# The first seven-product pair of a macaron block's feed-forward layer: two weight chunks fetched ahead into idle tiles, modulation rows fetched later, a shorter look-ahead

## The chip, the cores and the metric

The kernel runs on one core of one Trainium2 chip. A core has five instruction engines here: TensorE (PE in the profile, with its weight loads as PEld), VectorE (DVE), ScalarE (ACT), GpSimd (POOL) and SyncE (SP), which only issues transfers. Each engine takes its instructions strictly in the order of its own list, and waits on semaphores for the others. The metric is the device time of one execution in microseconds (us).

## The reference, cut to what matters

One transformer block on 512 tokens of width 1024, in float32. The change lies in the first of its three sub-layers, a SwiGLU feed-forward layer behind a modulated RMSNorm:

```
mod = silu(c) @ w_ada + b_ada                  # nine rows of 1024: shift, scale, gate, three times
u = modulate(rmsnorm(h, g_norm_ffn1), sh1, sc1)
a, b = split(u @ w_ffn1_in, 2)                 # 1024 -> 2 x 2816
h = h + 0.5 * gt1 * ((silu(a) * b) @ w_ffn1_out)
...                                            # token mixing, with gt2
...                                            # the second feed-forward layer, with gt3
return rmsnorm(h, g_final)
```

## The kernel before

**Tiles.** The hidden width 2816 is cut into 22 tiles of 128 columns, numbered j. Tile j needs 128 columns of the a half and 128 of the b half of `w_ffn1_in`. The layer runs in parts: tiles 0 to 3 are multiplied with `w_ffn1_out` first, then 4 to 7, and so on. Tiles 0 to 5 are made by plain products. From tile 6 on, two tiles (a pair) are made together by `duo`, as one 2 by 2 block product with seven block products in place of eight: the two halves of the width and the two halves of the tokens (T1, T2) are the blocks, some operands are sums and differences of blocks, and the seven results are combined in the banks A, B and C of PSUM. Pair 6 (tiles 6 and 7) is the first of them. Its products stand right behind the output products of part 0, and pair 8 follows.

**High and low parts.** A weight chunk (128 x 1024, 512 KB) is loaded raw, and then split: ACT rounds it into `whi` (line 321), DVE subtracts that from it into `wlo` (line 335). Each product is three groups of matmuls: high weights with high data, high with low, and last low weights with high data. A chunk listed in `self.outer` has its low part made in another way, which spares DVE: ACT writes the negated rounded chunk into `wlo` (line 317), and a transfer issued by POOL adds the chunk from memory onto it (line 319, `accum_op`). I call that an adding transfer. `whi` and `wlo` are rings of about seven chunks.

**The seven weights of a pair.** Four raw chunks r11, r12, r22, r21 are loaded in that order, and seven operands are made from them in place, in two buffers X besides; I number them w0 to w6:

```
for need, src, make in ((0, r11, None), (1, x0, (x0, r12, r11)), (2, x1, (x1, r22, x0)), (3, r21, None),
                        (3, r12, (r12, r22, r12)), (3, r22, None), (3, x0, (x0, r21, x1))):
```

The subtractions (`make`) are DVE's, at line 260. For pair 6, w0, w3 and w5 are listed in `self.outer`; for the later pairs w3 and w5 only.

**The buffers.** `fetch` hands a free buffer to the next chunk of the list and issues its load on SP's queue (line 244); `split` goes through the list up to a given place; `look(ahead)` does both for the current place plus `ahead`. At first there are three raw buffers. A buffer is free again when the last operand that is made from it has been split. The X buffers of pair 6 are still in use by the sums of the data (`u_steps`, tiles X, SH, SL: a list `todo` of seven steps, one behind each update of H in the output loop of part 0), and only then, when `todo` is empty, `hold` is dropped and w1 and w2 are made.

**Modulation rows.** `bg` consumes one row of `w_ada` (line 389) at places between the products, and `bg_fetch` issues the loads of the rows ahead (line 381), into the tiles `ada` at first, and from part 0's output products on into `cs` and `AR`. The rows 16 to 23 make the gate of this layer, which multiplies every output before it is added to H.

**In `duo`.** Before each product `look` is called, the product is issued, then what follows it: behind the first product ACT copies bank A into bank C (line 776), since A goes on to be accumulated and both are needed; behind that, the last data block is split (`first()`: UH, UL). `later(n, f)` puts f behind the n-th product from now; `ffn_post` uses it for the first token half of tiles 4 and 5 (line 677, 678), which nobody needs before part 1's outputs.

Of the kernel before, what the change touches and what calls it, by code (L numbers as in the profile page):

```python
# [8 lines left out]
F32 = mybir.dt.float32  # L9
F32R = mybir.dt.float32r  # L10
I32 = mybir.dt.int32
AF = mybir.ActivationFunctionType
OP = mybir.AluOpType

P = 128
T = 512
HT = 256
D = 1024
# [124 lines left out]
class Kernel:  # L143
# [6 lines left out]
    def plan(self):  # L150
        (i1, o1), mix, (i2, o2) = chunk_widths()
        self.chunks = []
        for name, ws in (("wf1i", i1), ("wf1o", o1), ("wmix", mix), ("wf2i", i2), ("wf2o", o2)):
            off, rec = 0, []
            for w in ws:
                rec.append((name, off, w))
                off += P * w
            self.chunks.append(rec)
        f1i, f1o, mx, f2i, f2o = self.chunks


        self.loads, self.order, self.last = [], [], {}
        self.shifted, self.outer, self.tail = set(), {}, []

        def plain(recs):
            for r in recs:
                n = len(self.loads)
                self.loads.append(r)
                self.last[n] = len(self.order)
                self.order.append((r[2], n, ("raw", n), None))  # L170

        def blocks(recs, outer=0, rest=()):
            n = len(self.loads)
            if outer > 1:
                self.outer.update({len(self.order) + 3: n + 3, len(self.order) + 5: n + 2})
            if outer in (1, 3):
                self.outer[len(self.order)] = n
            self.shifted.update(range(len(self.order), len(self.order) + 7 + len(rest)))
            self.loads.extend(recs)
            r11, r12, r22, r21 = (("raw", n + i) for i in range(4))  # L180
            x0, x1 = ("x", 0), ("x", 1)
            for need, src, make in ((0, r11, None), (1, x0, (x0, r12, r11)), (2, x1, (x1, r22, x0)), (3, r21, None),
                                    (3, r12, (r12, r22, r12)), (3, r22, None), (3, x0, (x0, r21, x1))):
                if rest and make == (x0, r21, x1):
                    self.tail.append(len(self.order))
                    plain(rest)
                for j, x in enumerate((r11, r12, r22, r21)):
                    if x == src or (make and x in make):
                        self.last[n + j] = len(self.order)
                self.order.append((D, n + need, src, make))  # L190

        def shift(i):

            self.shifted.update(range(len(self.order) - i, len(self.order)))

        def ffn(n, ins, outs, first):
            j, at = first, 0
            if first:
                plain(ins[:KT])
                at = KT  # L200
            for part, (k0, k1) in enumerate(PARTS):
                while j < pairs_before(n, part):
                    if j < PLAIN[n]:
                        plain(ins[at:at + 2])
                        if n and j < 2:
                            shift(2)
                        j, at = j + 1, at + 2
                    else:
                        blocks(ins[at:at + 4], 2 if j > PLAIN[n] else 3)
                        j, at = j + 2, at + 4  # L210
                recs = outs[part * KT // 2:(part + 1) * KT // 2]
                if part + 1 == len(PARTS):
                    continue
                if n or part:
                    blocks(recs, (3, 0, 2)[n], outs[-2:] if part + 2 == len(PARTS) else ())
                else:
                    base = len(self.order)
                    plain(recs)
                    self.outer.update({base + i: self.order[base + i][1] for i in (2, 3)})

        ffn(0, f1i, f1o, FIRST)
        base = len(self.order)
        plain(mx)
        self.shifted.update(range(base, base + 4))
        self.outer.update({i: self.order[i][1] for i in (base + 2, base + 3)})
        shift(2)
        ffn(2, f2i, f2o, 0)
        self.fetched = self.done = self.made = 0
        self.pos, self.held, self.retired, self.half, self.hold = 0, None, [], None, True
        self.at, self.start, self.top = {}, {}, 0  # L230
        self.buf = {}
        self.units = {base + i: 2 * P for i in (4, 5)}
        self.units.update({base + i: T for i in range(16, 20)})
# [434 lines left out]
    def ffn_post(self, j, s, pb, between=None):  # L668
        nc = self.nc
        h = self.kept[j // 2 % 3][:, j % 2 * T:j % 2 * T + T]  # L670
        nc.vector.tensor_tensor(h, s, pb, op=OP.mult)
        hh, hl = self.hh(j)
        t = slice(0, HT)
        if self.nh == 6 and j < 2:
            hh, hl, h = hh[:, t], hl[:, t], h[:, t]
        if self.nh == 4 and j in (4, 5):
            self.later(5, lambda: nc.scalar.activation(hh[:, t], h[:, t], AF.Copy))
            self.later(6, lambda: nc.vector.tensor_tensor(hl[:, t], h[:, t], hh[:, t], op=OP.subtract))
            return
        nc.scalar.activation(hh, h, AF.Copy)  # L680
        low = lambda: nc.vector.tensor_tensor(hl, h, hh, op=OP.subtract)
        if between is None:
            return low()
        between(low)
# [88 lines left out]
    def duo(self, j, first):  # L773

        nc, v = self.nc, self.nc.vector
# [5 lines left out]
        for i in range(3):  # L781
            h, l = self.S[i]
# [23 lines left out]
        for i, (bank, u, start) in enumerate(((A, blk(lo4, T1), True), (B, S[0], True), (A, S[1], False),  # L806
                                              (C, blk(hi4, T1), False), (A, S[2], False), (B, S[3], False),
                                              (A, blk(hi4, T2), False))):
            if i == 6:
                v.tensor_tensor(c1, c1, u3, op=OP.add)  # L810
            self.look(3 + i // 3 if first and self.nh == 6 else 5)
            self.product(bank, u, start)
            self.step()
            if i == 0:
                copy(C, A)
                if first:
                    first()
                    self.free.append(self.rawx[0])
            elif i == 1:
                copy(c1, r(B))  # L820
            elif i == 2:
                copy(c0, r(A))
            elif i == 3:
                silu(0, C)
            elif i == 4:
                copy(u3, r(A))
            elif i == 6:
                silu(1, A)
                v.tensor_tensor(c0, r(B), c0, op=OP.add)
            self.beside(j, i)  # L830
            if self.nh == 4 and j >= PARTS[-2][0] and self.todo:
                self.todo.pop(0)()
# [306 lines left out]
    def ffn(self, n, j, last=None):  # L1139
# [12 lines left out]
        for part, (k0, k1) in enumerate(PARTS[:-1]):  # L1152
            while j < pairs_before(n, part):
                if j < PLAIN[n]:
                    self.ffn_pair(j, beside)
                    j += 1
                else:
                    if j == k1:
                        if n and part == 0:
                            self.open_G()  # L1160
                        self.h_sums(k0, 0 if n else 4)
                    self.duo(j, last)
                    last = None
                    j += 2
# [18 lines left out]
            nk = k1 - k0  # L1183
            hk = [self.hh(k) for k in range(k0, k1)]
            for m in range(0, KT, 2):
                self.look(4 - m // 2)
                w = self.take()
                bs = [self.nb(), self.nb()]
# [18 lines left out]
    def beside_out(self, part):  # L1207

        if part == 0:

            assert not self.adat
            self.ada_pool.close()
            self.ada_free, self.ada_stop = [self.cs, self.AR], 40
            self.bg_fetch()
            self.sums = self.open_sums()
            self.open_G()
            self.todo, last = self.u_steps(0)
            return last
        if part == len(PARTS) - 2:
            assert self.ada_next == 40 and not self.adat, self.ada_next  # L1220
            self.ada_free = None
            self.retired = self.rawx
            self.free = [b for b in self.free if not any(b is x for x in self.rawx)]
            assert not self.todo
            self.trig_spread()
        if part == 2:
            self.todo = self.trig()
# [641 lines left out]
```

## Time and profile before

| what | value |
|---|---|
| time, median of 3 runs (lowest to highest) | 997.5 us (995.49 to 997.6) |
| the profiled execution: its own time, and its span from first to last instruction | 996.86 us, 995.1 us |
| granted TensorE clock, mean over the span | 0.993 |
| PE busy | 977.1 us (98%) |
| DVE busy | 829.1 us (83%) |
| ACT busy | 592.6 us (60%) |
| POOL busy | 97.2 us (10%) |
| transfers | 173.29 MB, mean 174 GB/s |

A row of a timeline or of the chain of waits begins with its start in microseconds from the span's start, then its duration. L770 is the matmul line of the block products, L366 to L368 are those of the plain ones. In the timeline, what stands in brackets at the end is the idle time of the engine just before the row, and who ended it. A row with x8 is eight instructions in a run.

### The profile page before, as it was taken

To read this page: it belongs to the slowest core of one execution; us is meant where nothing else is said; L and a number is where in the kernel's file an instruction comes from. 1 tells how busy PE (TensorE), PEld (TensorE's weight loads), DVE (VectorE), ACT (ScalarE), POOL (GpSimd) and SP (SyncE) were. 2 spreads that over 40 slices of the span, in tenths; PEclk is the share of its full clock that TensorE was granted. 3 is DMA by queue.
4 is the path that set the end of the run, shared out by engine and by line. 5 is a ranking of instruction groups with operands and counts; after the bars stand their busy time and mean duration, and the time that the engine had idled before them with its cause. 6 is when DMAs were issued, how large, how long until landed. Compare 5 with 4: busy or idle time off the path is not lost.

```text
span 995.1 us, 17672 instructions
## 1 busy us (share of the span) xinstructions
PE 977.1 (98%) x7106; PEld 920.1 (92%) x7106; DVE 829.1 (83%) x1244; ACT 592.6 (60%) x912; POOL 97.2 (10%) x109
## 2 busy tenths in 40 slices
PE   8999799999999999999999999999999999999997
PEld 6888799999999999889988888899999999999996
DVE  6976899999999876879667777579997988989875
ACT  6453577776868853334324333368776768677775
POOL 0001111111111100006300000001110011011001
PEclk9999899999999999999999999999999999999998
DMA  9869597777869723232255874345576666657632
GB/s 341 277 210 277 129 274 187 231 221 172 233 189 245 193 70 100 70 105 88 95 200 187 284 236 162 106 149 129 148 166 182 162 153 168 188 134 188 173 59 85
DMA packets 53924, 173.29 MB, mean 174 GB/s; under 512 B 6097, under 2 KB 11217, under 8 KB 53842
## 3 DMA queue, kind: packets, MB, share of 16 engines
q1 hardware_dynamic: 41778, 137.95, 40.3%
q0 software_dynamic: 11376, 33.56, 20.2%
q8 instruction: 55, 0.90, 0.4%
q10 hardware_dynamic: 688, 0.66, 0.2%
q14 instruction: 27, 0.22, 0.1%
HBM read 169.37 MB, written 2.77 MB: 173 GB/s over the span
## 4 chain that ended last, share of the span: by engine, by line
PE 90%; DVE 5%; ACT 2%; DMA 2%; issue 1%; DVEq 0%; ACTq 0%; SPq 0%
PE bank L770 34%; PE bank L366 7%; PE bank L368 7%; PE bank L367 7%; PE bank L890 6%; PE bank L892 6%; PE bank L891 6%; PE bank L632 3%; PE bank L1799 1%; PE bank L1801 1%; PE bank L1803 1%; PE bank L1389 1%; DMA ada<-wada 1%; PE bank L1570 1%; PE bank L1571 1%
## 5 line engine op out<-in xcount | busy, mean ns | idle before, releaser
L321 ACT ACTIVATE whi<-raw 128x1024 fp32r<-128x1024 f32 (+5 forms) x166 | 145.5, 896 | 9.6 <-DVE raw L260 5.0
L335 DVE TENSOR_TENSOR wlo<-raw,whi 128x1024 fp32r<-128x1024 f32 (+5 forms) x114 | 119.1, 1058 | 38.4 <-ACT whi L321 38.1
L321 ACT ACTIVATE whi<-X 128x1024 fp32r<-128x1024 f32 (+3 forms) x102 | 97.9, 973 | 31.1 <-DVE X L260 30.7
L335 DVE TENSOR_TENSOR wlo<-X,whi 128x1024 fp32r<-128x1024 f32 (+1 forms) x76 | 86.9, 1149 | 12.8 <-ACT whi L321 12.7
L366 PE MATMUL bank<-UH,whi 128*128 128x512 f32 x240 | 97.4, 406 | 0.0
L368 PE MATMUL bank<-UH,wlo 128*128 128x512 f32 x240 | 93.6, 390 | 0.0
L367 PE MATMUL bank<-UL,whi 128*128 128x512 f32 x240 | 93.5, 390 | 0.0
L770 PE MATMUL bank<-UH,whi 128*128 128x256 f32 x576 | 77.3, 277 | 0.0
L770 PE MATMUL bank<-UL,whi 128*128 128x256 f32 x576 | 77.2, 276 | 0.0
L770 PE MATMUL bank<-UH,wlo 128*128 128x256 f32 x576 | 77.2, 276 | 0.0
L770 PEld LDWEIGHTS bank<-UH,whi 128*128 128x128 f32 x576 | 71.1, 188 | 0.1
L770 PEld LDWEIGHTS bank<-UH,wlo 128*128 128x128 f32 x576 | 70.8, 188 | 0.0
L770 PEld LDWEIGHTS bank<-UL,whi 128*128 128x128 f32 x576 | 70.8, 188 | 0.0
L890 PE MATMUL bank<-HI,whi 128*128 128x256 f32 x240 | 66.8, 278 | 0.0
L891 PE MATMUL bank<-HK,whi 128*128 128x256 f32 x240 | 66.4, 277 | 0.0
L892 PE MATMUL bank<-HI,wlo 128*128 128x256 f32 x240 | 66.4, 277 | 0.0
L770 PE MATMUL bank<-SH,whi 128*128 128x256 f32 x432 | 59.2, 280 | 5.7 <-ACT bank L776 3.6
L389 DVE SCALAR_TENSOR_TENSOR ada<-ada,cond 128x1024 f32<-128x1024 f32 (+1 forms) x49 | 57.5, 1198 | 8.2 <-DMA ada<-wada 8.2
L770 PEld LDWEIGHTS bank<-SH,whi 128*128 128x128 f32 x432 | 53.9, 190 | 6.4 <-ACT bank L776 3.8
L890 PE MATMUL bank<-ut,whi 128*128 128x256 f32 x216 | 59.7, 277 | 0.0
L891 PE MATMUL bank<-G,whi 128*128 128x256 f32 x216 | 59.7, 277 | 0.0
L892 PE MATMUL bank<-ut,wlo 128*128 128x256 f32 x216 | 59.7, 277 | 0.0
(365 smaller groups left out, 2638.7 us busy)
## 6 DMA issues: line engine op xcount, KB each, us to landing
ada<-wada SPq DMA_DIRECT2D x47, 512.0 KB, 5.5
raw<-wmix SPq DMA_DIRECT2D x44, 512.0 KB, 4.4
raw<-wf1i SPq DMA_DIRECT2D x31, 512.0 KB, 6.9
raw<-wf2i SPq DMA_DIRECT2D x27, 512.0 KB, 5.2
wlo<-wf2i POOLq DMA_DIRECT2D x20, 512.0 KB, 6.0
AR<-wada SPq DMA_DIRECT2D x16, 512.0 KB, 4.0
raw<-wf1o SPq DMA_DIRECT2D x15, 512.0 KB, 5.4
X<-wf2i SPq DMA_DIRECT2D x14, 512.0 KB, 6.4
```

The lines of the kernel that those rows point to most:

```text
L321: self.nc.scalar.activation(self.hi[:, y], r[:, x], AF.Copy)
L335: self.nc.vector.tensor_tensor(self.lo[:, y], r[:, x], self.hi[:, y], op=OP.subtract)
L366: M(ps, hi, uh, start=start, stop=False)
L367: M(ps, hi, ul, start=False, stop=False)
L368: M(ps, lo, uh, start=False, stop=stop)
L389: self.nc.vector.scalar_tensor_tensor(t[:, c], t[:, c], 1.0, self.cond[:, c], op0=OP.mult, op1=OP.mult, accum_out=o)
L632: M(banks[j][:, hs], w[j][k][x], (self.UH, self.UL)[y][k][:, hs], start=h == k == x == y == 0, stop=k == KT - 1 and x == 1, skip_group_che ...
L770: M(bank[:, p * HT:(p + 1) * HT], w[4 * p + k][x], u[k][y], start=start and x == y == p == k == 0, stop=x == 1 and k == 3, skip_group_chec ...
L890: M(o, hi, uh, start=start and m % 2 == 0 and k == 0, stop=False, skip_group_check=True)
L891: M(o, hi, ul, start=False, stop=False, skip_group_check=True)
L892: M(o, lo, uh, start=False, stop=k == 1, skip_group_check=True)
L1389: M(o, pt[:, blk * P:blk * P + P], v, start=i == 0, stop=i == len(srcs) - 1)
```

## The change

Five edits, all at or around pair 6:

1. The third output chunk of part 0 is no longer in `self.outer`: its low part is made by DVE.
2. While the output products of part 0 run, two more buffers are handed out for raw chunks: `kept[1]`, whose tiles 2 and 3 have been used by then, and the first 1024 columns of tile G, which is opened for its own use (`open_G`) only when pair 8 begins. Being `retired`, they are given back after one use.
3. `bg_fetch` for the rows 24 and 25 (into `cs` and `AR`) moves from the beginning of that loop to its third step (m = 4).
4. The look-ahead in pair 6 is 3, 3, 3, 4, 4, 4, 5 chunks for its seven products in place of 5 for each.
5. The splits of tiles 4 and 5 (first token half) move two products back.

```diff
@@ plan: the output chunks of part 0
-                    self.outer.update({base + i: self.order[base + i][1] for i in (2, 3)})
+                    self.outer[base + 3] = self.order[base + 3][1]
@@ ffn_post
         if self.nh == 4 and j in (4, 5):
-            self.later(5, lambda: nc.scalar.activation(hh[:, t], h[:, t], AF.Copy))
-            self.later(6, lambda: nc.vector.tensor_tensor(hl[:, t], h[:, t], hh[:, t], op=OP.subtract))
+            self.later(7, lambda: nc.scalar.activation(hh[:, t], h[:, t], AF.Copy))
+            self.later(8, lambda: nc.vector.tensor_tensor(hl[:, t], h[:, t], hh[:, t], op=OP.subtract))
@@ duo
-            self.look(3 + i // 3 if first and self.nh == 6 else 5)
+            self.look(3 + i // 3 if first else 5)
@@ ffn, ahead of pair 8
-                        if n and part == 0:
+                        if part == (0 if n else 1):
                             self.open_G()
@@ ffn, the output loop of part 0
             for m in range(0, KT, 2):
+                if m == 4:
+                    self.bg_fetch()
                 self.look(4 - m // 2)
@@ beside_out
             self.ada_free, self.ada_stop = [self.cs, self.AR], 40
-            self.bg_fetch()
             self.sums = self.open_sums()
-            self.open_G()
+            self.retired = [self.kept[1], self.fw.tile([P, 3 * T], F32, name="G")[:, :D]]
+            self.free.extend(self.retired)
```

What this does to the instructions shows best on two engines. The first is SP's queue, from the last output chunk of part 0 (wf1o) on; wf1i are the chunks of pair 6 and then of pair 8, wada the modulation rows. Before:

```order
L244 DMA raw0_66<-wf1o 128x1024
L381 DMA ada_632<-wada 128x1024
L381 DMA ada_635<-wada 128x1024
L244 DMA raw1_67<-wf1i 128x1024
L381 DMA ada_670<-wada 128x1024
L244 DMA raw2_68<-wf1i 128x1024
L381 DMA cs_93<-wada 128x1024
L381 DMA AR_86<-wada 128x1024
L244 DMA raw0_66<-wf1i 128x1024
L244 DMA raw1_67<-wf1i 128x1024
L244 DMA X_123<-wf1i 128x1024
```

and now, from the last gate row on:

```order
L381 DMA ada_668<-wada 128x1024
L244 DMA raw2_68<-wf1i 128x1024
L244 DMA raw0_66<-wf1i 128x1024
L244 DMA kept1_121<-wf1i 128x1024
L244 DMA G_721<-wf1i 128x1024
L381 DMA cs_93<-wada 128x1024
L381 DMA AR_86<-wada 128x1024
L244 DMA raw1_67<-wf1i 128x1024
```

r21, the fourth chunk of pair 6, went into raw1 behind r11, which had to be used up first; now it goes into `kept1`, and r11 of pair 8 into G. The rows for `cs` and `AR` stand behind the four chunks.

The second is ACT around the first product of pair 6. Before, from the high parts of w1 and w2 on (`whi<-X`, two in a row):

```order
L321 ACTIVATE whi_69<-X_123 128x1024 x2
L317 ACTIVATE wlo_70<-raw1_67 128x1024
L321 ACTIVATE whi_69<-raw1_67 128x1024
L321 ACTIVATE whi_69<-raw2_68 128x1024
L677 ACTIVATE HI_118<-kept2_122 128x256 x2
L776 ACTIVATE bank6_103<-bank4_101 128x512
L736 ACTIVATE UH_81<-X_123 128x4x256
L317 ACTIVATE wlo_70<-raw0_66 128x256
L317 ACTIVATE wlo_70<-raw0_66 128x768
```

and now:

```order
L317 ACTIVATE wlo_70<-kept1_121 128x1024
L321 ACTIVATE whi_69<-kept1_121 128x1024
L776 ACTIVATE bank6_103<-bank4_101 128x512
L736 ACTIVATE UH_81<-X_123 128x4x256
L321 ACTIVATE whi_69<-raw2_68 128x1024
L776 ACTIVATE kept0_120<-bank5_102 128x2x256
L317 ACTIVATE wlo_70<-raw0_66 128x256
L317 ACTIVATE wlo_70<-raw0_66 128x768
L321 ACTIVATE whi_69<-raw0_66 128x256
L321 ACTIVATE whi_69<-raw0_66 128x768
L677 ACTIVATE HI_118<-kept2_122 128x256 x2
```

The copy of bank A into bank C (bank6 from bank4) now has only the two instructions of w3 between itself and the high parts of w1 and w2; the high part of w4 (from raw2) and the two splits of tiles 4 and 5 have moved behind it. TensorE's list is the same before and after, matmul for matmul.

## The prediction

> **What bounds the kernel now.** I read the page first, then PE's waits, then PE's timeline at the place where it waits. The page: who is busy, and PE's busy tenths in 40 slices of 24.9 us.
>
> ```profile
> PE 977.1 (98%) x7106; PEld 920.1 (92%) x7106; DVE 829.1 (83%) x1244; ACT 592.6 (60%) x912; POOL 97.2 (10%) x109
> PE   8999799999999999999999999999999999999997
> ```
>
> PE is the bound nearly everywhere; only the first, the fifth and the last slice show a hole. The fifth (99.5 to 124.4 us) holds the first products of pair 6. The waits of PE between 60 and 200 us, and the timeline there (start, duration):
>
> ```profile
> PE bank L770 <- ACT bank L776: 3.6, 1, 3.6
> PE bank L770 <- ACT whi L321: 2.1, 1, 2.1
> ...
> 101.20 0.39 PE L368 MATMUL bank<-HI,wlo 128*128 128x512 f32 x1
> ...
> 104.14 1.10 PE L770 MATMUL bank<-UH,whi 128*128 128x256 f32 x8
> 106.03 1.10 PE L770 MATMUL bank<-UH,wlo 128*128 128x256 f32 x8
> 109.21 1.19 PE L770 MATMUL bank<-SH,whi 128*128 128x256 f32 x8 [2.08 <-ACT whi L321]
> 111.19 1.09 PE L770 MATMUL bank<-SH,wlo 128*128 128x256 f32 x8
> 115.86 2.08 PE L770 MATMUL bank<-SH,whi 128*128 128x256 f32 x8 [3.58 <-ACT bank L776]
> 121.14 1.16 PE L770 MATMUL bank<-UH,whi 128*128 128x256 f32 x8
> ```
>
> A product is 24 matmuls. The first runs from 104.14 to 107.13, the second, after a wait of 2.08 for the high part of w1, from 109.21 to 112.28, the third, after 3.58 for the copy of bank A, from 115.86 to 121.14. What three products should take stands in the chain of waits, where 336 of them run unbroken:
>
> ```profile
> 79.59 12.34 DMA ada<-wada
> 92.02 1.24 DVE ada L389 x2
> ...
> 105.02 0.66 DVE H L1197
> ...
> 106.85 1.24 DVE X L260
> 108.15 3.42 DMA raw<-wf1i
> ...
> 170.41 38.19 PE bank L770 x336
> ```
>
> 38.19 / 336 is 0.1137 us for a matmul, 2.73 for a product, 8.19 for three. They took 17.00 (104.14 to 121.14). So **8.81 us is all that there is to win here**: 2.08 and 3.58 of waiting, 2.55 in the third product (5.28 in place of 2.73), and 0.6 in the first two (2.99 and 3.07). Why the third took twice its time is in the busy times of two stretches of 6.83 us (PE, PEld, DVE, ACT, POOL, then the granted clock):
>
> ```profile
> 107.63:114.45 6.82, 3.06 (x24) 2.87 (x24) 5.82 (x6) 4.92 (x5) 0.87 (x1) 1.00 0.44 154
> 114.45:121.28 6.83, 5.42 (x25) 5.42 (x26) 5.22 (x6) 6.78 (x12) 1.76 (x2) 0.50 0.91 183
> ```
>
> After a stretch in which PE worked 3.06 of 6.82 us, half the clock was granted for the next. Shorter waits take that away too.
>
> The same chain says who is late. The last row of the gate lands 12.34 us after its issue, DVE takes it at 92.02, and from then on DVE works without a break through the updates of H and the sums of the data up to 106.85, where it makes w1; the buffer that this frees lets r21 be loaded at 108.15, and ACT, in its order, waits for it:
>
> ```profile
> 108.11 1.06 ACT L321 ACTIVATE whi<-X 128x1024 fp32r<-128x1024 f32 x1 [5.58 <-DVE X L260]
> 109.42 1.06 ACT L321 ACTIVATE whi<-X 128x1024 fp32r<-128x1024 f32 x1 [0.26 <-DVE X L260]
> 111.65 1.06 ACT L317 ACTIVATE wlo<-raw 128x1024 fp32r<-128x1024 f32 x1 [1.17 <-DMA raw<-wf1i]
> 112.62 2.09 ACT L321 ACTIVATE whi<-raw 128x1024 fp32r<-128x1024 f32 x2
> 114.62 0.70 ACT L677 ACTIVATE HI<-kept 128x256 fp32r<-128x256 f32 x2
> 115.23 0.58 ACT L776 ACTIVATE bank<-bank 128x512 f32<-128x512 f32 x1
> 115.74 1.03 ACT L736 ACTIVATE UH<-X 128x1024 fp32r<-128x1024 f32 x1
> 116.68 1.14 ACT L317 ACTIVATE wlo<-raw 128x256 fp32r<-128x256 f32 x2
> ```
>
> **The change part by part.** *The adding transfer that goes (edit 1).* The two queues of the page, plain loads and adding transfers: packets, MB, share of all 16 transfer engines.
>
> ```profile
> q1 hardware_dynamic: 41778, 137.95, 40.3%
> q0 software_dynamic: 11376, 33.56, 20.2%
> DVE ada L389 <- DMA ada<-wada: 8.2, 3, 4.4
> ```
>
> 20.2% of 995.1 us for 33.56 MB is 5.99 us per MB: 0.524 MB cost 3.14 us of all engines, where a plain chunk costs 1.52. One such transfer, ahead of the last gate row, goes, so the row should land 3.1 us earlier. Bounds: 0 (it stood behind other traffic) and the 3.3 from which the output products hold DVE: the bank of H's seventh update is done at 101.59 (101.20 + 0.39), and w1 begins 1.83 behind that update (105.02 to 106.85), at 103.5 at best. I take 3.1: w1 at 103.75. DVE pays one more low part, at most 1.3 us in two pieces, while it waits up to 4.4 at a time for these rows (the third row above, from DVE's waits of 58 to 155 us): nothing. Without that cover it would be 1.3 of the 3.1, and 1.8 would be left.
>
> *First wait.* The high part of w1 ends 2.32 after DVE begins w1 (106.85 to 109.17): at 106.07, before PE is through with the first product (107.13). The 2.08 go. That holds as long as the row gains 2.08.
>
> *Second wait (edits 2, 4, 5).* r21 is loaded into `kept1`, straight behind r22, long before its use: ACT's 1.17 go. The high part of w2 starts 2.57 behind w1 (106.85 to 109.42), at 106.32, and ends at 107.38; the two instructions of w3 stand at 0.97 each (111.65 to 112.62), so the copy of bank A starts at 109.24 and ends at 109.82. PE, starting the second product at 107.13 with its 3.07, is through at 110.20: 0.38 to spare, the 3.58 go. If the row gains only 2.08, the copy ends at 110.84, and 0.7 stay. What moved behind the copy: w4's high part, then starting near 110.7, needed at 115.9; the splits of tiles 4 and 5, needed by part 1's outputs alone. w1's and w2's low parts are DVE's next:
>
> ```profile
> 109.25 2.50 DVE L335 TENSOR_TENSOR wlo<-X,whi 128x1024 fp32r<-128x1024 f32 x2
> ```
>
> They end 4.9 behind w1, at 108.65; w2's low third is due at 112.0. Four more instructions of 1.25 at most lie between that and w4's low part, at about 113.7, due at 117.7.
>
> *What is late next.* The low parts of w3 and w5 come by adding transfers, and these do not move up as far as PE does. POOL's issues of both in the trace (first and last start), and the times to landing of each; last those of all 44 and more up to 345 us:
>
> ```profile
> L319 POOL DMA_DIRECT2D wlo<-wf1i x1: 872/872/872, 113.1 to 113.1; - x1
> DMA to landing us min/median/max: 5.3/5.3/5.3
> ...
> L319 POOL DMA_DIRECT2D wlo<-wf1i x2: 865/943/1021, 117.4 to 118.2; - x2
> DMA to landing us min/median/max: 5.9/7.3/8.7
> ...
> DMA to landing us min/median/max: 2.9/6.8/10.5
> ```
>
> w3: issued 0.4 after ACT's instruction (111.65 + 1.06 = 112.71 to 113.1). Now that instruction runs from 107.30 to 108.36, so the issue is at 108.7, the landing at 114.0, or 115.0 if the two loads released by w1 (3.42 each) overlap it by a microsecond. The fourth product starts at 110.20 + 2.73 = 112.93, its last third at 114.75. I take a wait of 0.2; bounds 0 (2.9) and 4.45 (10.5).
>
> w5: behind the copy ACT splits UH (to 110.7), w4 (to 111.7), copies a bank (to 112.2) and then does w5's two pieces; POOL issued the second 1.5 behind ACT's start (116.68 to 118.2), now at 113.7, and 8.7 later, at 122.4, it lands. PE begins the sixth product at 115.86 + 2.73 = 118.6 and needs that piece at its third low matmul, at 120.65. **A new wait of 1.75**; bounds 0 (2.9) and 3.55 (10.5). I take 8.7, since that is this very transfer.
>
> [...]
>
> *Modulation rows later (edit 3).* `cs` and `AR` went behind the last gate row, so they don't delay it either way; their landing is due only at the first `bg` of pair 6. 0; a late landing would hold DVE there.
>
> *The clock.* Two waits of 0.2 and 1.75 leave PE at work for well over 3.06 of any 6.83 us; I take no halving. If the waits reach the 3.76 us idle of the row above, it is 2.55 more.
>
> *Later.* The gain must survive to the end. Busy times from pair 8's end to the end of the layer:
>
> ```profile
> 151.00:345.00 194.00, 194.00 (x1712) 194.00 (x1711) 183.14 (x236) 148.64 (x215) 30.76 (x35) 1.00 0.79 208
> ```
>
> PE has no hole, DVE is at 94%, so an earlier start goes through.
>
> **The sum**: 2.08 + 3.58 + 2.55 + 0.60 = 8.81, less 0.60 (the slow pace of the first two products, which nothing in the change touches), 0.2 and 1.75: 6.26. The profiled execution took 996.86 us (span 995.1), which makes 990.6; the median shown is 0.64 higher, so I say 990.8.
>
> **The rivals.** (B) *Full recovery*: w5's transfer lands in 6.8, the median, or less: 8.81 - 0.6 = 8.2, 988.7. For it: with four chunks loaded ahead, fewer loads compete; against: both pieces wait in one queue, behind each other. [...]
> (C) *The gate row lands no earlier*, so the edit's main step does nothing: w1 stays at 106.85 and the 2.08 stay; the copy comes 3.1 later than above, at 112.92, 0.6 after the second product; w5's piece at 125.5 against 123.2: 2.3. Gain 8.81 - 0.6 - 2.08 - 0.6 - 2.3 = 3.2: 993.6. For it: the row's 12.34 us are shared with other traffic, an adding transfer among it that stays.
> (D) *The adding transfer of w3 takes the longest time seen*, 10.5: 4.45 of wait, half the clock again (2.55), nothing left for w5: gain 1.2, 995.7.
> (E) *Slower*, by the same transfer alone: at 14 us from issue the wait is 7.95, with 2.55 and 0.6 that is 11.1 against 8.81: 999.1. It decides from about 13.7 us; the longest row is 10.5, which speaks against it.
>
> **How the numbers follow.** 0.2% (2 us) is about what can be told from no change. The forecast of 990.8 (989.5 to 992.5 for bounds of half a wait) gets 0.57, B 0.17, C 0.13, D 0.07, E 0.03, other things 0.03. Range 988.0 to 994.6: it takes in B and C and leaves out D and E. Faster: forecast, B and C, and a little of D, 0.89; within 0.2%: the rest of D, 0.07; slower 0.04.
>
> **What would show it.** In the new profile the chain has no load of wf1i between w1 and pair 6's products; DVE takes the last gate row near 89; the 2.08 and 3.58 are gone, and no half clock stands near 115. A wait of one to two microseconds on a POOL transfer stands in the sixth product, near 120.7; pair 6 ends near 125.8 in place of 132.1. The prediction is wrong if that row does not move, if the copy of bank A still ends a wait, or if a wait of over 3 us stands at w3 or w5.

## The result, and the profile after

The changed kernel takes 990.64 us, the median of seven runs (988.7 to 993.53), against 997.05 (994.84 to 997.84) for the kernel before on the same chip: a ratio of 0.994, with a 95% interval of 0.992 to 0.996. The forecast was 990.8, in a range of 988.0 to 994.6.

The page of the profiled execution, whose own time was 993.37 us and its span 991.6, shows who was busy, PE's tenths, and the queue of the adding transfers:

```profile
PE 977.8 (99%) x7106; PEld 921.3 (93%) x7106; DVE 830.4 (84%) x1246; ACT 591.5 (60%) x910; POOL 95.6 (10%) x107
PE   8999999999999999999999999999999999999997
q0 software_dynamic: 11088, 33.04, 19.7%
```

The hole in the fifth slice is gone, and the adding queue moves 0.52 MB less. PE's waits between 60 and 200 us, and its timeline in pair 6 (the first rows of products one to four, then the whole sixth and the first row of the seventh) show what is left there:

```profile
PE bank L770 <- DMA wlo<-wf1i: 1.7, 1, 1.7
...
107.09 1.10 PE L770 MATMUL bank<-UH,whi 128*128 128x256 f32 x8
...
109.92 1.10 PE L770 MATMUL bank<-SH,whi 128*128 128x256 f32 x8
...
112.74 1.07 PE L770 MATMUL bank<-SH,whi 128*128 128x256 f32 x8
...
115.46 1.07 PE L770 MATMUL bank<-UH,whi 128*128 128x256 f32 x8
...
121.00 1.07 PE L770 MATMUL bank<-UH,whi 128*128 128x256 f32 x8
121.91 1.07 PE L770 MATMUL bank<-UL,whi 128*128 128x256 f32 x8
122.82 0.39 PE L770 MATMUL bank<-UH,wlo 128*128 128x256 f32 x2
124.95 0.96 PE L770 MATMUL bank<-UH,wlo 128*128 128x256 f32 x6 [1.75 <-DMA wlo<-wf1i]
125.75 1.07 PE L770 MATMUL bank<-UH,whi 128*128 128x256 f32 x8
...
128.47 0.73 PE L770 MATMUL bank<-UH,whi 128*128 128x256 f32 x5
```

The two waits of 2.08 and 3.58 are gone; the third product takes 2.72 (112.74 to 115.46) where it took 5.28. One wait stands there that was not there before: 1.75 us, in the sixth product, behind two low matmuls. The seven products end at 128.47, 21.38 us after they began; before they took 27.97 (104.14 to 132.11).

Pair 6 starts 2.95 us later than in the profile before, though. That has nothing to do with the change; it lies in the first 20 us, ahead of everything that was edited. PE's timeline there, before:

```profile
11.51 1.22 PE L1733 MATMUL bank<-ones,ut 128*128 128x1 f32 x8
...
15.18 1.50 PE L1728 MATMUL bank<-H,ones 128*128 128x128 f32 x12
16.93 2.14 PE L1799 MATMUL bank<-UH,whi 128*128 128x512 f32 x8 [0.25 <-ACT UH L486]
```

and after, with the same instructions two lines further down in the code:

```profile
11.56 1.71 PE L1735 MATMUL bank<-ones,ut 128*128 128x1 f32 x8
...
17.53 2.67 PE L1730 MATMUL bank<-H,ones 128*128 128x128 f32 x12
19.95 2.08 PE L1801 MATMUL bank<-UH,whi 128*128 128x512 f32 x8
```

Twelve matmuls that took 1.50 take 2.67. In the 14 profiles of this study (kernel before, changed kernel, and twelve runs below) the large matmuls begin between 16.2 and 17.6 us in nine, and between 19.5 and 20.0 in five. One kernel, the last of the table below, was profiled twice and had both (16.24 and 19.57). So the whole time of a single execution says little about a few microseconds. What follows goes by a stage: from the first matmul of pair 6 to the first one of part 1's outputs, fourteen block products in all. **It took 47.06 us before and takes 40.63 now, 6.43 less.** From there to the end of the span it is 843.88 and 843.87: what the stage gained went through to the end, as far as two decimals show.

Why the waits went is in the rows of DVE and ACT. DVE takes the last gate row and makes w1 and w2; ACT makes what follows:

```profile
89.68 1.23 DVE L389 SCALAR_TENSOR_TENSOR ada<-ada,cond 128x1024 f32<-128x1024 f32 x1 [1.56 <-DMA ada<-wada]
...
104.58 0.75 DVE L1199 SCALAR_TENSOR_TENSOR H<-bank,mod,H 128x512 f32<-128x512 f32 x1 [0.84 <-PE bank L368]
...
106.50 1.23 DVE L260 TENSOR_TENSOR X<-raw,raw 128x1024 f32<-128x1024 f32 x1
...
107.75 1.06 ACT L321 ACTIVATE whi<-X 128x1024 fp32r<-128x1024 f32 x1 [7.57 <-DVE X L260]
...
110.04 1.04 ACT L317 ACTIVATE wlo<-kept 128x1024 fp32r<-128x1024 f32 x1
110.99 1.05 ACT L321 ACTIVATE whi<-kept 128x1024 fp32r<-128x1024 f32 x1
111.93 0.58 ACT L776 ACTIVATE bank<-bank 128x512 f32<-128x512 f32 x1
```

DVE now waits for PE ahead of an update of H (0.84): it has caught up with the output products, and w1 starts 0.59 before pair 6 does (106.50 against 107.09), where it started 2.71 after it. r21 stands ready in `kept`, so ACT goes from w2 to w3 and to the copy of bank A without a wait; the copy ends at 112.51, 0.23 before the third product starts.

### The profile page after: what moved, and what is told of

It is laid out like the page before. It is cut to its first block, busy times and chain, and to the rows that moved or that the text cites. A ratio compares the mean times of both kernels' runs of the same rounds, so it can differ in the third digit from the quotient of the medians.

```text
span 991.6 us, 17667 instructions
## 1 busy us (share of the span) xinstructions
PE 977.8 (99%) x7106; PEld 921.3 (93%) x7106; DVE 830.4 (84%) x1246; ACT 591.5 (60%) x910; POOL 95.6 (10%) x107
## 4 chain that ended last, share of the span: by engine, by line
PE 94%; DVE 3%; ACT 1%; DMA 1%; issue 0%; DVEq 0%; ACTq 0%
PE bank L770 33%; PE bank L366 8%; PE bank L368 8%; PE bank L367 8%; PE bank L890 6%; PE bank L892 6%; PE bank L891 6%; PE bank L632 3%; PE bank L1801 1%; PE bank L1805 1%; PE bank L1803 1%; PE bank L1391 1%; PE bank L1572 1%; DMA wlo<-wf1i 1%; PE bank L1730 1%; PE bank L1573 1%
## 5 line engine op out<-in xcount | busy, mean ns | idle before, releaser
L335 DVE TENSOR_TENSOR wlo<-raw,whi 128x1024 fp32r<-128x1024 f32 (+5 forms) x117 | 121.6, 1053 | 38.4 <-ACT whi L321 38.1
L335 DVE TENSOR_TENSOR wlo<-X,whi 128x1024 fp32r<-128x1024 f32 (+1 forms) x74 | 84.5, 1148 | 11.9 <-ACT whi L321 11.8
L770 PE MATMUL bank<-UH,wlo 128*128 128x256 f32 x576 | 77.5, 277 | 1.7 <-DMA wlo<-wf1i 1.7
L770 PE MATMUL bank<-UH,whi 128*128 128x256 f32 x576 | 77.2, 276 | 0.0
L770 PE MATMUL bank<-UL,whi 128*128 128x256 f32 x576 | 77.2, 276 | 0.0
L770 PEld LDWEIGHTS bank<-UH,wlo 128*128 128x128 f32 x576 | 70.9, 188 | 1.9 <-DMA wlo<-wf1i 1.9
L770 PEld LDWEIGHTS bank<-UH,whi 128*128 128x128 f32 x576 | 70.9, 188 | 0.1
L770 PEld LDWEIGHTS bank<-UL,whi 128*128 128x128 f32 x576 | 70.8, 188 | 0.0
L770 PE MATMUL bank<-SL,whi 128*128 128x256 f32 x432 | 58.5, 278 | 0.0
L770 PE MATMUL bank<-SH,whi 128*128 128x256 f32 x432 | 58.3, 277 | 0.0
```

Of the source, the lines that this page charges most:

```text
L335: self.nc.vector.tensor_tensor(self.lo[:, y], r[:, x], self.hi[:, y], op=OP.subtract)
L770: M(bank[:, p * HT:(p + 1) * HT], w[4 * p + k][x], u[k][y], start=start and x == y == p == k == 0, stop=x == 1 and k == 3, skip_group_chec ...
```

## The experiments

Twelve runs, told in the order of the questions: what each edit is worth, what the wait that is left hangs on, and what it takes to remove it. The table has the time of the stage, the waits of PE in it, and for how long half the clock was granted there; each time is from one profile.

| kernel | stage, us | waits of PE, us | half clock, us |
|---|---|---|---|
| before | 47.06 | 2.08, 3.58 | 6.83 |
| changed | 40.63 | 1.75 | 0 |
| changed, profiled again | 42.35 | 2.00 | 3.41 |
| edit 1 taken back | 44.17 | 0.80, 0.63, 1.82 | 3.41 |
| edit 1 alone | 44.43 | 3.06 | 6.83 |
| edit 2 taken back | 41.95 | 0.98, 1.58 | 0 |
| edit 3 taken back | 40.63 | 1.53 | 0 |
| edits 4 and 5 taken back | 42.69 | 2.61 | 3.41 |
| edit 4 taken back | 42.71 | 1.99, 0.2 | 3.41 |
| edit 5 taken back | 43.07 | 0.27, 2.09 | 3.41 |
| w5 by DVE | 42.37 | 2.20, in pair 8 | 3.41 |
| two modulation rows later | 40.81 | 1.92 | 0 |
| both of these | 38.55 and 39.08 | none | 0 |

**Edit 1 taken back**: the third output chunk of part 0 gets its low part by an adding transfer again.

```diff
-                    self.outer[base + 3] = self.order[base + 3][1]
+                    self.outer.update({base + i: self.order[base + i][1] for i in (2, 3)})
```

> The changed kernel with edit 1 taken back: the third output chunk of part 0 gets its low part by an adding transfer again. Measured is the time from the first matmul of pair 6 to the first of part 1's outputs (pairs 6 and 8): 47.06 us before, 40.63 in the changed kernel. My theory (three waits, each with a cause of its own): the last gate row lands late again, w1 is made about 3 us later, the wait of about 2.1 ahead of the second product comes back, with 0.5 to 0.7 ahead of the third and some 0.5 more at w5: 43 to 44.5 us. Rival (the early load of r21 is all that counts): 40.6 us, with no wait ahead of the second product.

44.17. The last gate row's issue on SP's queue with its time to landing, then the start of w1 on DVE's timeline, and PE's waits in the stage:

```profile
L381 SPq DMA_DIRECT2D ada<-wada x1: 330/330/330, 79.4 to 79.4; - x1
DMA to landing us min/median/max: 11.1/11.1/11.1
...
105.33 1.23 DVE L260 TENSOR_TENSOR X<-raw,raw 128x1024 f32<-128x1024 f32 x1
...
PE bank L770 <- DMA wlo<-wf1i: 1.8, 1, 1.8
PE bank L770 <- ACT whi L321: 0.8, 1, 0.8
PE bank L770 <- ACT bank L776: 0.6, 1, 0.6
```

The row takes 11.1 us to land (12.34 before); in the changed kernel the slowest of the last three took 7.0. w1 starts 1.41 behind pair 6's start (103.92), in place of 0.59 ahead of it, and the first wait is back. It is 0.8 and not 2.1, since w1 is still 1.30 earlier against PE than before: without edit 1 the other edits bring that much, and which of them isn't shown. So 44.17 lies in my range by another sum, with 1.3 less in the first wait and with 3.41 us at half the clock, 1.7 us, which I hadn't counted. Rival C of the prediction (the row lands no earlier by this) falls.

**Edit 1 alone**, on the kernel before.

```diff
-                    self.outer.update({base + i: self.order[base + i][1] for i in (2, 3)})
+                    self.outer[base + 3] = self.order[base + 3][1]
```

> The kernel before with edit 1 alone. My theory, from the prediction's terms: the last gate row lands some 3 us earlier relative to pair 6, so the wait of 2.08 for the high part of w1 goes, but r21 still comes late into its buffer and ACT's copy of bank A behind it: the second wait stays at 3 to 4.5 us, with slow matmuls behind it or not: 44 to 45.5 against 47.06. Rival C of the prediction, for this edit by itself: the row lands no earlier and the time stays within 0.4 of 47.06.

44.43, with one wait, for the copy of bank A. PE's waits, and ACT's row for w3 from its timeline:

```profile
PE bank L770 <- ACT bank L776: 3.1, 1, 3.1
...
109.49 1.06 ACT L317 ACTIVATE wlo<-raw 128x1024 fp32r<-128x1024 f32 x1 [1.73 <-DMA raw<-wf1i]
```

The first wait is gone and the second stays, as the terms of the prediction have it: ACT still waits 1.73 for r21. The last gate row lands in 6.54 us here, and w1 starts at 104.11, 0.6 ahead of pair 6 (104.72), as in the changed kernel: edit 1 alone does the whole of that step.

**Edit 2 taken back** (r21 and r11 of pair 8 wait for buffers again).

```diff
-            self.retired = [self.kept[1], self.fw.tile([P, 3 * T], F32, name="G")[:, :D]]
-            self.free.extend(self.retired)
```

> The changed kernel with edit 2 taken back: no extra buffers, so r21 waits again until w1 has used up r11; the order on ScalarE stays the new one. My theory: the load goes out about 0.7 us behind the start of pair 6 and lands 3.4 later, ScalarE does w3's two instructions from 4.2 on, the copy of bank A ends at 6.7 and the third product, due at 5.65, waits 1.1 us, with as much more at w3's or w5's low part: 41.5 to 43 us for pairs 6 and 8. Rival (the early load is all that counts): the wait of 3.6 us and the half clock come back, 46 us or more.

41.95, with waits of 0.98 at the copy of bank A and 1.58 at w5, by PE's waits:

```profile
PE bank L770 <- DMA wlo<-wf1i: 1.6, 1, 1.6
PE bank L770 <- ACT bank L776: 1.0, 1, 1.0
```

The wait at the copy is near the 1.1 that I expected; the one at w5 is no longer than in the changed kernel. The stage is 1.32 longer, so the buffers are worth about a microsecond, and the rival falls: no half clock comes back.

**Edits 4 and 5 taken back** (look-ahead of 5, the splits of tiles 4 and 5 two products earlier).

```diff
-            self.look(3 + i // 3 if first else 5)
+            self.look(3 + i // 3 if first and self.nh == 6 else 5)
...
-            self.later(7, lambda: nc.scalar.activation(hh[:, t], h[:, t], AF.Copy))
...
+            self.later(5, lambda: nc.scalar.activation(hh[:, t], h[:, t], AF.Copy))
...
```

> The changed kernel with edits 4 and 5 taken back: look-ahead 5 in pair 6, the splits of tiles 4 and 5 at their old place; the two extra buffers stay. My theory: the copy of bank A stands behind w4's high part again, which needs a subtraction that VectorE does not finish before about 6.1 us behind the start of pair 6, and behind the two splits: it ends near 8.3, the third product waits about 2.7 us; 42 to 43.3 us for pairs 6 and 8. Rival (the early load of r21 is all that counts): 40.6 us.

42.69, and one wait of 2.61. ACT's rows ahead of the copy:

```profile
113.07 1.06 ACT L321 ACTIVATE whi<-raw 128x1024 fp32r<-128x1024 f32 x1 [1.28 <-DVE raw L260]
114.03 0.71 ACT L677 ACTIVATE HI<-kept 128x256 fp32r<-128x256 f32 x2
114.65 0.58 ACT L776 ACTIVATE bank<-bank 128x512 f32<-128x512 f32 x1
```

w4's high part costs the copy 1.06 and 1.28 of waiting for DVE besides, the two splits 0.7. No wait is left at w5: PE, held up by 2.61 and then by 3.41 us at half the clock, comes there late enough.

**Edit 4 alone taken back** (the first of the two pairs of lines above), to part these two.

> The changed kernel with edit 4 alone taken back (the look-ahead of 5 chunks for every product of pair 6). Compared by the time from the first matmul of pair 6 to the first of part 1's outputs: 47.06 us before, 40.63 changed, 42.69 with edits 4 and 5 both taken back (one wait of 2.61 for the copy of bank A). My theory: the high part of w4 stands ahead of that copy on ACT again and costs it 1.0 us and more, the two splits of tiles 4 and 5 (0.7 us) stay behind: a wait of 1.5 to 2.3 at the third product, 41.3 to 42.4. Rival: the splits are what matters, and the look-ahead does nothing: no wait at the third product, 1.75 at w5, 40.6.

42.71, a wait of 1.99 at the third product and one of 0.2 at w5. The wait is what I expected; the time is above my 42.4, since half the clock was granted for 3.41 us behind it (below).

**Edit 5 alone taken back** (the second pair of lines).

> The changed kernel with edit 5 alone taken back (the two splits of tiles 4 and 5, 0.70 us of ACT, stand ahead of the copy of bank A again). In the changed kernel that copy ended 0.23 before the third product began. My theory: a wait of 0.4 to 0.6 appears at the third product, and the wait at w5, whose transfer then starts no earlier, shrinks by as much: together 1.5 to 2.2, so the stage takes 40.5 to 41.0 us as in the changed kernel (40.63), or 1.7 more where half the clock is granted for 3.41 us: edit 5 is worth nothing by itself once the transfer of w5 is late. Rival: the two waits add up, 0.5 and 1.75 in full, 41.1 to 41.5, or 1.7 more with half the clock.

43.07. The theory fell and the rival held by its time, with the half clock: the two waits add up to 2.36, though one is 0.27 and the other 2.09. PE's waits, and POOL's issue of w5's two pieces from its timeline:

```profile
PE bank L770 <- DMA wlo<-wf1i: 2.1, 1, 2.1
PE bank L770 <- ACT bank L776: 0.3, 1, 0.3
...
112.91 1.79 POOL L319 DMA_DIRECT2D wlo<-wf1i  x2 [3.95 <-ACT wlo L317]
```

I had said that w5's transfer starts no earlier with the splits moved. It does: in the changed kernel the splits stand behind w5's two pieces. Here POOL issues w5 9.09 us after pair 6's start (112.91 - 103.82), in the changed kernel 8.49 after it (115.58 - 107.09).

These last three kernels all had half the clock for 3.41 us, as the changed kernel itself had when it was profiled again (42.35). Against that profile they are 0.34, 0.36 and 0.72 slower; against the first (40.63) 2.06, 2.08 and 2.44, most of which is the clock. Edits 4 and 5 take away a wait of 2.61 at the third product, but a wait of 1.75 or 2.00 at w5 stands in its place.

**Edit 3 taken back** (the modulation rows for `cs` and `AR` fetched at the start of the output loop).

```diff
-                if m == 4:
-                    self.bg_fetch()
...
+            self.bg_fetch()
```

> The changed kernel with edit 3 taken back: the loads of the modulation rows 24 and 25 stand ahead of the four chunks in SyncE's queue again. My theory: nothing waits for either, 40.6 us for pairs 6 and 8 (40.2 to 41). Rival (the rows hold up the chunks behind them): w2 or w3 comes late, and a wait of 0.5 to 2.5 us appears ahead of the second, third or fourth product, 41 to 43 us.

40.63, as the changed kernel, with a wait of 1.53: nothing that edit 3 does is seen here, and the rival falls.

**The wait that is left: w5 by DVE.** The low part of pair 6's w5 is subtracted by DVE.

```diff
-                self.outer.update({len(self.order) + 3: n + 3, len(self.order) + 5: n + 2})
+                self.outer[len(self.order) + 3] = n + 3
+                if (outer, self.nw5) != (3, 0):
+                    self.outer[len(self.order) + 5] = n + 2
+                self.nw5 += 1
```

> The changed kernel with one thing more: the low part of w5 of pair 6 is made by DVE and not by the adding transfer, whose landing ends the one wait that is left (1.75 us). Theory 1 (the transfer alone is late): the wait goes and nothing takes its place, 40.63 becomes 38.9. Theory 2, mine (DVE is the next bound of this stage): the wait goes, but the 1.25 us of DVE come out behind it, as a wait for DVE later in pair 6 or in pair 8: 40.0 to 40.9, no gain of over 0.6.

42.37, no gain: 1.74 over the first profile of the changed kernel, level with its second (42.35). Pair 6 has no wait at all, but pair 8's third product has one of 2.20. PE's waits, then ACT's between 110 and 135 us (here and with both edits below the lines stand three further down, so L773 is L770):

```profile
PE bank L773 <- ACT bank L779: 2.2, 1, 2.2
...
ACT whi L324 <- DVE X L263: 3.7, 2, 2.3
ACT whi L324 <- DVE raw L263: 2.3, 1, 2.3
```

ACT had waited for DVE ahead of the copy. But it had in the changed kernel too, where pair 8's copy of bank A ends 26.85 us after pair 6's start and its product begins at 26.91, with 0.06 to spare. Here the copy ends at 27.05, only 0.20 later; PE is there sooner, since it no longer waits at w5. Theory 2 held in that DVE is the next bound, at 21.27 busy of 22.90 us in the first part of the changed kernel's stage:

```profile
107.10:130.00 22.90, 21.15 (x183) 20.95 (x182) 21.27 (x23) 17.14 (x24) 3.52 (x4) 1.00 0.78 194
```

But it isn't 1.25 us more of DVE that comes out: a second wait stood right behind the first, hidden by it. The size was off by the half clock that the 2.20 brought with it, 1.7 us.

**Two modulation rows later, w5 as in the changed kernel.** The rows that DVE takes in pair 6 are taken in pairs 10 and 12.

```diff
-        if self.nh == 4 and i in (2, 5):
+        if self.nh == 4 and i in {6: (), 10: (0, 2, 5), 12: (0, 2, 5)}.get(j, (2, 5)):
```

> The changed kernel with the two modulation rows alone taken later; w5's low part comes by its adding transfer as before. Theory 1 (the transfer sets this wait, whatever DVE does): the wait of 1.75 at w5 stays, 40.2 to 41.2 us against 40.63. Theory 2 (DVE's load makes ACT and so POOL's issue late): the wait shrinks with DVE's load to under 0.8, 38.3 to 39.7. I hold the first: ACT's two instructions for w5 waited for no DVE instruction in the changed kernel.

40.81 with a wait of 1.92 at w5: the transfer sets this wait, not DVE's load.

**Both together.**

> The changed kernel with w5's low part of pair 6 made by DVE, as above, and the two modulation rows that DVE takes in pair 6 taken later, one each in pairs 10 and 12. If DVE is the next bound behind the transfer (my theory), this frees some 2.5 us of it and the stage comes near to the unbroken 14 products, 38.2 us: 38.3 to 39.4, where w5 by DVE alone gives 40.0 or more. Rival: the waits go elsewhere (the adding transfer of w3, the rows where they are taken now): 40 or more, or a longer time from part 1's outputs to the end than the 843.9 of both kernels.

38.55, and PE has no wait. The busy times from pair 6's first matmul to part 1's outputs:

```profile
103.82:142.37 38.55, 38.55 (x337) 38.43 (x336) 36.84 (x40) 32.72 (x44) 5.27 (x6) 1.00 0.76 196
```

Fourteen products at 2.73 are 38.2. Pair 8's copy of bank A ends 24.78 us after pair 6's start. Neither edit gains anything by itself; together they are worth 2.1 us.

**Both kernels timed on one chip.**

> The changed kernel again, timed on the chip of the next two. 990.6 and 0.6% under the kernel before by the earlier comparison: 988.7 to 993.5 for single executions, of which some 3 us hang on the start, where the full clock is granted earlier or later.

> The changed kernel with w5's low part of pair 6 by DVE and two modulation rows of pair 6 taken in pairs 10 and 12 (run before for one look, 38.55 us from pair 6's first matmul to part 1's outputs against 40.63, and no wait there). My theory: these 2.1 us go through to the end: a median of 988 to 989, 0.2% under the changed kernel timed beside it. Rival: the look was a fast start, and the 2.1 us are given back behind pair 8, where DVE takes the rows: the two medians within 0.7 us.

The changed kernel had a median of 992.85 (989.88 to 994.81, eight runs), 0.9956 of the kernel before (0.9939 to 0.9974); the version with both edits 990.58 (989.32 to 992.54, six runs), 0.9943 (0.9927 to 0.9958). I expected 990.6 and 988 to 989, too low: both came out some 2 us above that, and the profiled executions of both started late (19.72 and 19.57). The version with both edits stands 2.27 under the changed kernel, 0.23%, as the theory said, but the two intervals overlap: by whole times it isn't shown to be faster. By the stage it is: 38.55 and 39.08 against 40.63 and 42.35. Behind the stage its two profiles needed 842.40 and 844.57 us, the changed kernel's 843.87 and 843.84, so whether the two rows cost something where they are taken now stays open.

**The half clock, across all of them.** The changed kernel profiled a second time lost 1.72 more in the stage than the first time, with nearly the same wait (2.00 and 1.75). Busy times in stretches of 3.41 us, laid on the edges that the trace records for the clock (the granted clock is the sixth number behind the length; the first profile has full clock recorded from 19.95 to 985.92, which is 283 stretches of 3.413, and 3.41 is the shortest grant of half the clock in the table), first time:

```profile
122.35:125.76 3.41, 1.66 (x15) 1.47 (x14) 3.41 (x6) 2.02 (x4) 0.00 (x0) 1.00 0.91 324
125.76:129.18 3.42, 3.42 (x33) 3.42 (x32) 3.42 (x5) 1.75 (x2) 0.86 (x1) 1.00 0.33 46
```

second time:

```profile
122.05:125.47 3.42, 1.42 (x13) 1.22 (x12) 3.42 (x6) 2.02 (x4) 0.00 (x0) 1.00 0.92 318
125.47:128.88 3.41, 3.41 (x18) 3.41 (x18) 3.41 (x5) 1.78 (x2) 0.86 (x1) 0.50 0.34 58
```

and with edit 1 taken back:

```profile
120.72:124.13 3.41, 1.59 (x14) 1.39 (x13) 3.41 (x5) 2.01 (x3) 0.00 (x0) 1.00 1.03 335
124.13:127.55 3.42, 3.42 (x18) 3.42 (x18) 3.42 (x6) 2.20 (x3) 0.88 (x1) 0.50 0.18 52
```

Idle for 1.75 of such a stretch, PE kept its clock; idle for 1.82, it had half of it for the next 3.41 us, and 18 matmuls ran where 33 ran at full clock. In the stage, over all profiles of the table, the stretches at full clock with idle times of 1.75 or less (1.59, 1.13, 0.99, 0.98 and shorter) were followed by full clock, and those with 1.82, 1.87, 1.99, 2.01, 2.12, 2.13, 2.18 and 2.34 by half. Where the stretch at half clock had waits in it too (1.41 us in the kernel before, 0.93 with edit 1 alone), a second one at half followed, hence the 6.83 there; with 0.27 or less none did. This is shown for the stage alone, whose matmuls are all 256 columns wide. At the end of the program, where there are matmuls 128 columns and one column wide, a stretch of the changed kernel with 1.04 us idle (982.51 to 985.92) was already followed by half the clock. So what counted in the stage was how much of a wait fell into one stretch: the 1.92 us with the two rows later fell on an edge (0.78 and 1.13) and cost nothing more.

## Why the prediction was right

By its steps:

- *The gate row.* It said 3.1 us earlier, w1 from 103.75. The row landed in 7.04 us where it took 12.34 (82.54 to 89.58), and DVE took it 17.41 us ahead of pair 6's start (89.68 against 107.09) where it had been 12.12 (92.02 against 104.14): 5.29 earlier, so 3.1, the price from the queues' mean shares, was too low. w1 stands only 3.30 earlier, since DVE then waits for the output products (0.84 ahead of each of the last two updates of H before it): the prediction had put that bound 0.64 ahead of pair 6's start, and w1 came 0.59 ahead. So the step came out by its bound and not by its price. Edit 1 is its cause: alone on the kernel before it gives all of the 3.30. Without it the other edits give 1.30, and taking it back costs 2.00.
- *The two waits.* 2.08 and 3.58 went. The copy of bank A was to end 0.38 before it was needed; it ended 0.23 before.
- *The half clock of 2.55.* It went, in the first profile. "I take no halving" was the weak step: the new wait of 1.75 was measured against 3.76 us idle of 6.82, but in these profiles the stage kept its clock with 1.75 us idle of 3.41 and lost it with 1.82. The second profile had 2.00 there and lost 1.7. So the two profiles of this one kernel fall on both sides.
- *The slow pace, 0.60, which was said to stay.* Mis-sized: the first two products take 5.65 (107.09 to 112.74) against 5.46 at full pace, 0.19. The rest of the 0.60 went with the waits. By my estimate most of it was the end of the last matmul ahead of each: a row of two matmuls is 0.39 long where they start every 0.1137, which leaves 0.16, twice.
- *w3: 0.2 of wait.* None; its transfer landed in 5.4 us.
- *w5: 1.75 of wait, for 8.7 from issue to landing.* The wait came at that matmul, with 1.75 to two decimals, behind this transfer, by the chain of waits (start, duration):

```profile
116.32 8.59 DMA wlo<-wf1i
124.95 22.93 PE bank L770 x198
```

  In the second profile it was 2.00, and 1.53 and 1.92 in two kernels with the same work on ACT and POOL up to there. Two decimals are luck, the size is not. Rival B, full recovery with 6.8 us or less for this transfer, falls with it.
- *Edit 3 at 0, and the gain carried to the end*: both as said (40.63 without the edit; 843.88 and 843.87 behind the stage).

The sum was 6.26 for the stage, 6.43 was measured. So near a hit is partly luck, for its misses cancel: 0.41 of the slow pace and the 0.2 at w3 were saved as well, but from the fourth product to the end of the stage the kernel, without its wait, took 30.51 us (115.46 to 147.72, less 1.75) where it took 30.06 before (121.14 to 151.20). Subtracted from the median of 997.5, the sum would have said 991.2; the 990.8 lies between that and the 990.6 from the profiled execution. The stage alone would have brought the profiled execution of 996.86 to 990.4; its own 993.37 are that and 2.95 of a late start. That the median of the runs fell within 0.2 of the forecast owes something to how early and late starts were mixed, which the prediction did not know of: the second set of the changed kernel has its median at 992.85.

## What to carry to other kernels

When a tight stage loses a wait, look for the transfer whose issue did not move up as far as its consumer, and price it by the rows of that very transfer (8.59 us here), not by a typical one (6.8, the median before). In this stage a wait cost some 1.7 us more than its length where 1.82 us of it or more fell into one stretch of 3.41, so two runs of one order can differ by more than the edit under test (40.63 and 42.35 here): compare a stage between two of its own instructions, not the whole time. And where two resources are nearly bound together (here a late transfer, and DVE at 93%), relieving one may bring nothing until the other is relieved too: look how much the next wait has to spare.

## What the runs showed of the hardware that was not expected

In this stage half the clock followed shorter waits than the 3.76 us idle of 6.82 that the prediction went by: 1.75 us idle of 3.41 kept the full clock, 1.82 lost it, at a price of 1.7 us (18 matmuls in place of 33, at 0.1137 each). In none of these stages was a stretch of 3.41 us at full clock idle for more than 2.34.

The start of one and the same program varied by 3 us: with both edits the large matmuls begin at 16.24 in one profile and at 19.57 in the other. With edit 1 alone the trace records the half clock there:

```profile
13.70:17.10 3.40, 3.40 (x16) 3.40 (x17) 2.30 (x8) 1.78 (x3) 0.00 (x0) 0.50 1.04 407
```

In the profile of the changed kernel the clock's records only begin at 19.95 (at 12.05 in that of the kernel before), and that its slow matmuls ahead of that ran at half the clock is inferred from their durations (2.67 against 1.50), not shown.

Two things stay open. In some runs the matmuls of a stage without any wait start every 0.118 us and not every 0.1137 (eight in 0.94 where 0.91 is usual), which is most of what lies between 38.55 and 39.08. And behind the stage three of the twelve runs needed 842.4 to 842.5 us to the end where the others needed 843.6 to 844.6; no run here tells why.
